# A residual turned by TensorE instead of by VectorE and a scratch in HBM

## The chip, the core and the metric

The kernel runs on one core of one Trainium2 chip. The time is what one execution takes on the device, in microseconds (us). A core has a matrix engine (TensorE, PE in the profile), three engines for elementwise work (VectorE or DVE, ScalarE or ACT, GpSimd or POOL), and a sync engine (SyncE or SP) that here only issues transfers (DMAs). Each engine runs its own list of instructions strictly in the listed order and waits on semaphores for the others. ACT issues DMAs too; such an instruction stands in ACT's list, and what is behind it waits for its turn. Data live in SBUF (128 partitions, the working memory), in PSUM (8 banks, where matmuls put their results) and in HBM.

## The reference, cut to what matters

The program is a two-layer decoder trunk on 512 tokens of width 1024. The change lies at its very end, in the last step of the last layer and the final norm:

```python
def per_layer_embed(h, p_i, g_norm, w_in, w_gate, b_gate):
    gate = jax.nn.sigmoid(rmsnorm(h, g_norm) @ w_gate + b_gate)
    return (p_i @ w_in) * gate
...
        h = h + conv_ffn(rmsnorm(h, norm_ffn[i]), f_w_up[i], f_conv_w[i], f_conv_b[i], f_w_down[i])
        h = h + per_layer_embed(h, p[i], norm_ple[i], ple_w_in[i], ple_w_gate[i], ple_b_gate[i])
...
    return rmsnorm(h, norm_final)
```

`h` is the residual. Its last use needs `h` twice: split into two parts as the operand of the gate matmul, and as itself in the addition `h + ...`.

## The kernel before

**Layout.** The residual is kept with features on the partitions: eight tiles `h[0]` to `h[7]`, each 128 features by 512 tokens. The last gate is computed the other way round, tokens on the partitions: four token blocks `i` of 128 tokens, each 1024 features wide, in two halves `c` of 512. So the residual has to be turned, from 8 tiles of features into 4 blocks of tokens (`hT[i][c]`), before the gate can be added to it.

**Matmuls in three products.** Each float32 operand is split into a high part that TensorE takes in its fast format and the low rest. A product of two split operands is three matmuls (`mm3`, L222 to L224, and `mm3t`, L233 to L235, which has tokens on the output's partitions). One gate half of one block is 8 x 3 = 24 matmuls of 128x512.

**Weights.** They come from HBM in units of 128x1024 (`load`, issued by SP into six buffers `r0` to `r5`), are cast to their high part by ACT (`wh`, L187) and have the rest taken by DVE (`wl`, L196), into four pairs of buffers `wh`/`wl`. A unit's cast needs its transfer and a free `wh` buffer; a transfer needs a free `r` buffer, that is the cast and the subtraction of the unit six places ahead. The names carry the unit's number: units 187 to 194 are the last down projection of the second layer, two for each quarter of the output; 195 to 198 are the gate's first half; 199 to 206, of 128x512, are its second half and go to buffers of their own (`own_ah`, `own_al`).

**The last down projection** (`dense_add`, L366) makes `d0` to `d7` in PSUM, 21 matmuls each. DVE adds each to the residual (`h`, L383); `norm.take` then has ACT make the high part of the gate's operand (`np10h`, L280) and its square (`np1sq`, L309), DVE the low part (`np10l`, L281), and POOL the running sum of squares (`np1acc`, L314). Behind this it calls `then`, which is `turn_h` (L963): DVE turns the tile within each 32x32 square (`ht`, a STREAM_TRANSPOSE, L966), and one tile later `write` (L956) issues four DMAs on ACT's list (L960), which put the squares to their places in a scratch `rows` in HBM. SP reads the scratch back as `hT` (L992), two transfers a block.

**The last gate** (`half` and `finish`, L1044 and L1053). `ms` is four small matmuls that put the tokens' sums of squares on the partitions; DVE and POOL make the root `rt` of it (L355, L357). For each half: matmuls into a PSUM bank `gate`, `z` on DVE (L1010, reads the bank, and needs `rt`), a sigmoid on ACT (`gs`, L1016), two operations on DVE (`gs` L1017 and `hT` L1019, which adds to the turned residual), a square with its sum on ACT (L1029). For each block: `total` on DVE (L1033, L1034), a root on POOL (`rfin`, L1039), a scaling on DVE (L1058); blocks 0 and 1 are turned back on DVE (L1064) and stored in sixteen DMAs (L1067), block 2 is stored as it is (L1061). The last block is cut finer: its second half is two quarters (`gate7`, `gate8`), and its end is the chain `z`, `gs`, `hT`, a sum on DVE (L1093), a root on POOL, a scaling on DVE and ACT (L1100, L1102), and two DMAs (L1103).

**What sets the order.** Code is written in program order, and a scheduler merges it into one list for each engine by priorities and by when it thinks that operands are ready. So an edit at one place can move instructions of others. PSUM tiles of one bank come from the tags `mm` (four banks), `tr` and `pv`; the pair of banks `sc` (`psum2`) exists once. Up to the first two tiles of the last down projection every engine's list is the same in both kernels.

Of the kernel before, what the change touches and what calls it, by code (L numbers as in the profile page):

```python
# [14 lines left out]
P = 128  # L15
# [37 lines left out]
def tile_yoco(ctx: ExitStack, tc: tile.TileContext, t, out: bass.AP, out_b: bass.AP):  # L53
# [18 lines left out]
    def psum2(name):  # L72
        return mmp.tile([P, 2, S], F32, tag="sc", name=name)
# [81 lines left out]
    def load(upto, queue=nc.sync):  # L155
        while state["raw"] < min(upto, len(units)):
            j = state["raw"]
            a, m, _ = units[j]
            tags = state["tags"]
            r = wp.tile([P, UNIT], F32, tag=f"r{tags[state['turn'] % len(tags)]}", bufs=1, name=f"wraw{j}")  # L160
            state["turn"] += 1
            if len(a.shape) == 4:
                for c in range(2):
                    queue.dma_start(r[:, :m].rearrange("p (k c n) -> p k c n", c=2, n=256)[:, :, c], a[:, :, c])
            else:
                queue.dma_start(r[:, :m], a)
            raws[j] = r
            state["raw"] += 1
# [57 lines left out]
    def mm3t(ps, xs, parts, c0, n, tok, first=True, last=True):  # L226

        for k, ((wh, wl, off), (xh, xl)) in enumerate(zip(parts, xs)):
            a, b = off + c0, off + c0 + n
            s = slice(tok * P, (tok + 1) * P)  # L230
            st = first and k == 0
            en = last and k == len(parts) - 1
            nc.tensor.matmul(ps, xh[:, s], wh[:, a:b], start=st, stop=False)  # L233
            nc.tensor.matmul(ps, xl[:, s], wh[:, a:b], start=False, stop=False)
            nc.tensor.matmul(ps, xh[:, s], wl[:, a:b], start=False, stop=en)  # L235
# [59 lines left out]
    class Norm:  # L295
# [56 lines left out]
    def inv_root(ms, name, scale=1.0):  # L352
        n = ms.shape[1]
        m = const.tile([P, n], F32, tag=f"ms{n}", bufs=2, name=f"{name}m")
        nc.vector.tensor_scalar(m, ms, scale, EPS, op0=ALU.mult, op1=ALU.add)  # L355
        r = const.tile([P, n], F32, tag=f"rt{n}", bufs=2, name=f"{name}rt")
        nc.gpsimd.tensor_tensor(r, m, minus_half[:, :n], op=ALU.pow)  # L357
        return r
# [7 lines left out]
    def dense_add(xs, kk, norm, fresh=False, then=None):  # L366

        for c in range(4):
            parts = chunk(256, kk)
            pss = []  # L370
            if fresh and c == 0:
                pss = [psum(f"d{j}") for j in range(2)]
                for k0, k1 in ((0, kk - 1), (kk - 1, kk)):
                    for j in range(2):
                        mm3(pss[j], parts[k0:k1], xs[k0:k1], j * P, first=k0 == 0, last=k1 == kk)
            for j in range(2):
                m = 2 * c + j
# [5 lines left out]
                nc.vector.tensor_add(h[m], h[m], ps)  # L383
                if norm is not None:
                    norm.take(m)
                if then is not None:
                    load(state["unit"] + RAWS)
                    then(m)

    def ffn(l, norm, nxt, then=None):  # L390
# [559 lines left out]
        nf.take(m)  # L950

    npl = Norm("np1", [(xp, "x", gain("norm_ple", 1))])
    rows = dram.tile([S, D], F32, name="rows")
    queue = []

    def write(m, t):  # L956

        for q in range(P // SQ):
            c0 = m * P + q * SQ
            nc.scalar.dma_start(rows[:, c0 : c0 + SQ].rearrange("(b i) j -> i b j", i=SQ),  # L960
                              t[q * SQ : (q + 1) * SQ, :].rearrange("p (b j) -> p b j", j=SQ))

    def turn_h(m):  # L963

        t = tp.tile([P, S], F32, tag=f"c{m % 2}", name=f"ht{m}")
        nc.vector.transpose(t, h[m])  # L966
        if queue:
            write(*queue.pop())
        queue.append((m, t))

    ffn(1, nf, npl, turn_h)
    write(*queue.pop())

    xs = npl.xs[0][0]
    brow, grow = (mp.tile([P, D], F32, tag=tag, name=f"row_{tag}") for tag in ("m4", "m5"))
    for i, r in enumerate((brow, grow)):
        nc.sync.dma_start(r.rearrange("p (m q) -> p m q", m=KD), lines[:, i, :].partition_broadcast(P))
    turned_h = at.tile([P, NC - 1, S], F32, tag="vd", name="hT")
    hT = [turned_h[:, q, :] for q in range(NC - 1)] + [at.tile([P, S], F32, tag="alibi", name="hT3")]
    hT = [hT[:2], hT[2:]]  # L980
# [63 lines left out]
    def half(i, c):  # L1044

        if c == 0 and i < 2:
            ps = pss[i]
        else:
            ps = psum(f"gate{i}_{c}")
            mm3t(ps, xs, parts2 if c else parts, 0, S, i)  # L1050
        square(i, gated(i, c * S, S, ps, c), c)

    def finish(i):  # L1053

        mean(i, 2, total[:, i : i + 1])
        r = root(i)
        for c in range(2):
            nc.vector.scalar_tensor_tensor(hT[i][c], hT[i][c], r, grow[:, c * S : (c + 1) * S],  # L1058
                                           op0=ALU.mult, op1=ALU.mult)
            if i == 2:  # L1060
                nc.sync.dma_start(out_b[0, :, c * S : (c + 1) * S], hT[i][c])  # L1061
                continue
            t = tp.tile([P, S], F32, tag=f"c{c}", name=f"y{i}_{c}")
            nc.vector.transpose(t, hT[i][c])  # L1064
            for q in range(P // SQ):
                s0 = i * P + q * SQ
                nc.sync.dma_start(flat[c * S : (c + 1) * S, s0 : s0 + SQ].rearrange("(f c) a -> c f a", c=SQ),  # L1067
                                  t[q * SQ : (q + 1) * SQ, :].rearrange("p (f a) -> p f a", a=SQ))
# [101 lines left out]
```

## Time and profile before

| | us |
|---|---|
| median of three runs | 1144.76 (1144.58 to 1144.79) |
| the profiled execution | 1144.59 |
| its span, first to last instruction | 1142.9 |
| PE busy | 1123.6 (98%) |
| DVE busy | 736.2 (64%) |
| ACT busy | 505.4 (44%) |
| POOL busy | 134.6 (12%) |
| TensorE clock granted, mean | 0.994 |

The profiled execution lies within the runs; 1.69 us of its time are outside its span. A row of the timeline has the start in us from the span's beginning, the duration in us, the engine, the line of the kernel, the operation, and output `<-` inputs by the program's names; "x4" is four merged into one row, and in brackets stands the time the engine sat idle before it and whose work ended that. "ACTq" and "SPq" are the parts of ACT and SP that issue DMAs. A matmul's duration overlaps that of the next: what it costs is the distance from its start to the next start. PEclk is the granted TensorE clock, 1.00 at full speed.

### The profile page before, as it was taken

To read this page: it belongs to the slowest core of one execution; us is meant where nothing else is said; L and a number is where in the kernel's file an instruction comes from. 1 tells how busy PE (TensorE), PEld (TensorE's weight loads), DVE (VectorE), ACT (ScalarE), POOL (GpSimd) and SP (SyncE) were. 2 spreads that over 40 slices of the span, in tenths; PEclk is the share of its full clock that TensorE was granted. 3 is DMA by queue.
4 is the path that set the end of the run, shared out by engine and by line. 5 is a ranking of instruction groups with operands and counts; after the bars stand their busy time and mean duration, and the time that the engine had idled before them with its cause. 6 is when DMAs were issued, how large, how long until landed. Compare 5 with 4: busy or idle time off the path is not lost.

```text
span 1142.9 us, 13466 instructions
## 1 busy us (share of the span) xinstructions
PE 1123.6 (98%) x5116; PEld 932.2 (82%) x5116; DVE 736.2 (64%) x974; ACT 505.4 (44%) x801; POOL 134.6 (12%) x160
## 2 busy tenths in 40 slices
PE   9999999999999999999999999999999999999895
PEld 7888888888888888888898887888888888888675
DVE  7356467762677367557858887677636773677556
ACT  6533344441343244445756776544413432344342
POOL 2100210000000000022235564100000000000101
PEclk9999999999999999999999999999999999999998
DMA  9322322322323333332054324433223233323443
GB/s 319 110 94 81 104 89 96 111 92 92 109 69 100 111 109 88 99 111 94 18 147 129 93 93 166 136 104 111 86 98 103 73 102 111 102 70 113 90 124 74
DMA packets 70097, 120.66 MB, mean 106 GB/s; under 512 B 30344, under 2 KB 41104, under 8 KB 70032
## 3 DMA queue, kind: packets, MB, share of 16 engines
q1 hardware_dynamic: 52704, 117.24, 32.5%
q10 hardware_dynamic: 17328, 2.56, 1.2%
q8 instruction: 40, 0.66, 0.2%
q14 instruction: 25, 0.20, 0.1%
HBM read 110.33 MB, written 4.20 MB: 100 GB/s over the span
## 4 chain that ended last, share of the span: by engine, by line
PE 93%; DVE 2%; DMA 1%; issue 1%; ACT 1%; ACTq 0%; SPq 0%; POOL 0%; POOLq 0%
PE up L222 14%; PE up L224 14%; PE up L223 14%; PE d L224 8%; PE d L223 8%; PE d L222 8%; PE o L222 1%; PE q L222 1%; PE o L223 1%; PE o L224 1%; PE sc L738 1%; PE q L224 1%; PE gate L222 1%; PE q L223 1%; PE u L222 1%
## 5 line engine op out<-in xcount | busy, mean ns | idle before, releaser
L196 DVE TENSOR_TENSOR wl<-wraw,wh 128x1024 fp32r<-128x1024 f32 (+2 forms) x197 | 239.5, 1218 | 117.9 <-ACT wh L187 117.3
L187 ACT CAST wh<-wraw 128x1024 fp32r<-128x1024 f32 (+1 forms) x196 | 201.7, 1032 | 245.9 <-PE d L223 132.8
L224 PE MATMUL d<-ah,wl 128*128 128x512 f32 x352 | 137.8, 391 | 2.2 <-DVE wl L196 2.2
L223 PE MATMUL d<-al,wh 128*128 128x512 f32 x352 | 137.6, 391 | 0.0
L222 PE MATMUL d<-ah,wh 128*128 128x512 f32 x352 | 137.5, 391 | 0.0
L222 PE MATMUL up<-nf00h,wh 128*128 128x512 f32 x352 | 137.1, 390 | 0.0
L222 PE MATMUL up<-nf10h,wh 128*128 128x512 f32 x352 | 137.0, 389 | 0.0
L224 PE MATMUL up<-nf00h,wl 128*128 128x512 f32 x352 | 137.0, 389 | 0.0
L223 PE MATMUL up<-nf00l,wh 128*128 128x512 f32 x352 | 136.9, 389 | 0.0
L224 PE MATMUL up<-nf10h,wl 128*128 128x512 f32 x352 | 136.9, 389 | 0.0
L223 PE MATMUL up<-nf10l,wh 128*128 128x512 f32 x352 | 136.9, 389 | 0.0
L412 ACT ACTIVATE c<-hs,vec 128x512 f32<-128x512 f32 x88 | 71.8, 816 | 88.9 <-DVE hs L408 87.9
L413 DVE SCALAR_TENSOR_TENSOR c<-hs,vec,c 128x511 f32<-128x511 f32 x88 | 65.9, 748 | 37.4 <-ACT c L412 37.2
L383 DVE TENSOR_TENSOR h<-h,d 128x512 f32<-128x512 f32 x56 | 38.4, 686 | 79.7 <-PE d L224 79.7
L224 PEld LDWEIGHTS d<-ah,wl 128*128 128x128 f32 x352 | 66.4, 189 | 16.4 <-DVE wl L196 2.6
L222 PEld LDWEIGHTS d<-ah,wh 128*128 128x128 f32 x352 | 66.5, 189 | 13.9
L223 PEld LDWEIGHTS d<-al,wh 128*128 128x128 f32 x352 | 66.4, 189 | 13.9
L284 ACT CAST ah<-a 128x512 fp32r<-128x512 f32 x44 | 27.4, 622 | 113.5 <-DVE a L418 113.5
L224 PEld LDWEIGHTS up<-nf10h,wl 128*128 128x128 f32 x352 | 66.1, 188 | 13.8
L222 PEld LDWEIGHTS up<-nf00h,wh 128*128 128x128 f32 x352 | 66.1, 188 | 13.7
L223 PEld LDWEIGHTS up<-nf00l,wh 128*128 128x128 f32 x352 | 66.1, 188 | 13.7
L223 PEld LDWEIGHTS up<-nf10l,wh 128*128 128x128 f32 x352 | 66.1, 188 | 13.7
(289 smaller groups left out, 1976.1 us busy)
## 6 DMA issues: line engine op xcount, KB each, us to landing
wraw<-in_w_up SPq DMA_DIRECT2D x88, 512.0 KB, 3.5
wraw<-in_w_down SPq DMA_DIRECT2D x32, 512.0 KB, 3.5
wraw<-in_w_down SPq DMA_DIRECT2D x16, 384.0 KB, 3.3
wraw<-in_w_u SPq DMA_DIRECT2D x8, 512.0 KB, 7.7
wraw<-in_w_out SPq DMA_DIRECT2D x8, 512.0 KB, 3.5
wraw<-in_w_gate SPq DMA_DIRECT2D x8, 512.0 KB, 3.8
wraw<-in_w_q SPq DMA_DIRECT2D x8, 512.0 KB, 3.5
wraw<-in_w_o SPq DMA_DIRECT2D x8, 512.0 KB, 3.2
```

The costliest lines, as they stand in the source:

```text
L187: nc.scalar.copy(wh[:, :n], src)
L196: nc.vector.tensor_sub(wl[:, :n], src, wh[:, :n].bitcast(F32))
L222: nc.tensor.matmul(ps, wh[:, a:b], xh, start=st, stop=False)
L223: nc.tensor.matmul(ps, wh[:, a:b], xl, start=False, stop=False)
L224: nc.tensor.matmul(ps, wl[:, a:b], xh, start=False, stop=en)
L284: nc.scalar.copy(hi, src)
L383: nc.vector.tensor_add(h[m], h[m], ps)
L412: nc.scalar.activation(c, hs, AF.Identity, bias=v("conv_b", l * 2 * NJ + col), scale=cw[2])
L413: nc.vector.scalar_tensor_tensor(c[:, 1:], hs[:, : S - 1], cw[1], c[:, 1:], op0=ALU.mult, op1=ALU.add)
L738: nc.tensor.matmul(o[:, e, 2 * P - nk :], q, x[g // 2][:, g % 2, t0 : t0 + nk], start=st, stop=not st)
```

## The change

The turned residual is made another way. `turn_h`, `write`, the scratch `rows` and the eight reads of it are gone. In their place a new `turn_h(i)` turns one token block: eight TensorE transposes (a matmul with the identity, 128x128 each, in float32), one from each `h[k]`, into the pair of banks `sc`, and one ACT copy of 128x1024 from there to SBUF. It is called once ahead of the gate's second halves (block 0) and then behind the second half of block `i` for block `i + 1`. Since `sc` exists once, a block's transposes wait for the copy of the block before.

What comes with it: `dense_add` no longer calls `load` ahead of `then`; `ms` moves from `sc` to the bank `tr`; the blocks of the gate are now run one after the other (first half, second half, finish) and not both first halves first; the turned block lies in buffers `r3` to `r5`; and the output of blocks 0 and 1 is turned into one tile of 128x1024 and stored in eight DMAs of double size instead of sixteen.

```diff
@@ dense_add
                 if then is not None:
-                    load(state["unit"] + RAWS)
                     then(m)
@@ behind the last attention
-    rows = dram.tile([S, D], F32, name="rows")
-    queue = []
-
-    def write(m, t):
-
-        for q in range(P // SQ):
-            c0 = m * P + q * SQ
-            nc.scalar.dma_start(rows[:, c0 : c0 + SQ].rearrange("(b i) j -> i b j", i=SQ),
-                              t[q * SQ : (q + 1) * SQ, :].rearrange("p (b j) -> p b j", j=SQ))
-
-    def turn_h(m):
-
-        t = tp.tile([P, S], F32, tag=f"c{m % 2}", name=f"ht{m}")
-        nc.vector.transpose(t, h[m])
-        if queue:
-            write(*queue.pop())
-        queue.append((m, t))
-
-    ffn(1, nf, npl, turn_h)
-    write(*queue.pop())
+    ffn(1, nf, npl)
...
-    for i in range(2):
-        r = wp.tile([P, D], F32, tag=f"r{4 + i}", bufs=1, name=f"hT{2 + i}")
-        hT.append([r[:, :S], r[:, S:]])
-    for i in range(NC):
-        for c in range(2):
-            nc.sync.dma_start(hT[i][c], rows[i * P : (i + 1) * P, c * S : (c + 1) * S])
-    ms = psum2("ms")[:, 0, :NC]
+    full += [wp.tile([P, D], F32, tag=f"r{2 + i}", bufs=1, name=f"hT{i}") for i in range(1, NC)]
+    hT = [[x[:, :S], x[:, S:]] for x in full]
+    def turn_h(i):
+
+        ps = psum2(f"ht{i}")
+        for k in range(KD):
+            nc.tensor.transpose(ps[:, k // 4, k % 4 * P : (k % 4 + 1) * P], h[k][:, i * P : (i + 1) * P], ident)
+        nc.scalar.copy(full[i], ps.rearrange("p a s -> p (a s)"))
+
+    ms = psum("ms", "tr")[:, :NC]
...
     rt = inv_root(ms, "np1", 1.0 / D)
+    turn_h(0)
@@ half
             mm3t(ps, xs, parts2 if c else parts, 0, S, i)
+        if c and i < end:
+            turn_h(i + 1)
         square(i, gated(i, c * S, S, ps, c), c)
@@ finish
-            t = tp.tile([P, S], F32, tag=f"c{c}", name=f"y{i}_{c}")
-            nc.vector.transpose(t, hT[i][c])
+            nc.vector.transpose(t[:, c * S : (c + 1) * S], hT[i][c])
+        if i < 2:
...
     for i in range(2):
-        half(i, 0)
-    for i in range(2):
-        half(i, 1)
+        for c in range(2):
+            half(i, c)
         finish(i)
```

Three places show what this does to the lists. A name here is the tile's, with its own number behind an underscore.

The first is DVE's list in the last down projection, where the low parts of the weights for `d6` and `d7` are made (`wl193`, `wl194`). Before:

```order
L383 TENSOR_TENSOR h4_84<-h4_84,d4_8500 128x512
L966 STREAM_TRANSPOSE ht4_8535<-h4_84 128x512
L281 SCALAR_TENSOR_TENSOR np10l3_6020<-h3_83,vec_79,np10h3_6019 128x512
L383 TENSOR_TENSOR h5_85<-h5_85,d5_8541 128x512
L966 STREAM_TRANSPOSE ht5_8570<-h5_85 128x512
L196 TENSOR_TENSOR wl193_8493<-wraw193_8383,wh193_8492 128x1024
L196 TENSOR_TENSOR wl194_8497<-wraw194_8385,wh194_8496 128x768
```

After:

```order
L383 TENSOR_TENSOR h2_82<-h2_82,d2_8397 128x512
L281 SCALAR_TENSOR_TENSOR np10l2_6018<-h2_82,vec_79,np10h2_6017 128x512
L196 TENSOR_TENSOR wl193_8458<-wraw193_8455,wh193_8457 128x1024
L383 TENSOR_TENSOR h3_83<-h3_83,d3_8426 128x512
L196 TENSOR_TENSOR wl194_8464<-wraw194_8461,wh194_8463 128x768
L281 SCALAR_TENSOR_TENSOR np10l3_6020<-h3_83,vec_79,np10h3_6019 128x512
L196 TENSOR_TENSOR own199_al4_8658<-wraw199_8654,own199_ah4_8657 128x512
L383 TENSOR_TENSOR h4_84<-h4_84,d4_8467 128x512
L196 TENSOR_TENSOR own200_al5_8665<-wraw200_8661,own200_ah5_8664 128x512
L281 SCALAR_TENSOR_TENSOR np10l4_6022<-h4_84,vec_79,np10h4_6021 128x512
L196 TENSOR_TENSOR wl195_8529<-wraw195_8525,wh195_8528 128x1024
L383 TENSOR_TENSOR h5_85<-h5_85,d5_8496 128x512
```

`wl193` stood behind the addition `h5`, which needs `d5`, the matmuls just ahead of those that need `wl193`; it now stands ahead of `h3`. In the same way `wl195`, for the gate's first matmuls, stood behind `h7` and now stands ahead of `h5`.

The second is ACT's list where the down projection ends. Before:

```order
L309 ACTIVATE np1sq6_8609<-h6_86 128x512
L960 DMA rows_6029<-ht5_8570 32x16x32 x4
L280 ACTIVATE np10h7_6027<-h7_87,vec_79 128x512
L309 ACTIVATE np1sq7_8650<-h7_87 128x512
L960 DMA rows_6029<-ht6_8619 32x16x32 x4
L960 DMA rows_6029<-ht7_8654 32x16x32 x4
L187 CAST wh197_8670<-wraw197_8445 128x1024
L187 CAST wh198_8674<-wraw198_8448 128x1024
L187 CAST own199_ah4_8716<-wraw199_8529 128x512
```

After:

```order
L309 ACTIVATE np1sq6_8564<-h6_86 128x512
L187 CAST own202_ah7_8678<-wraw202_8675 128x512
L187 CAST wh197_8605<-wraw197_8602 128x1024
L187 CAST own205_ah1_8699<-wraw205_8696 128x512
L187 CAST own206_ah2_8706<-wraw206_8703 128x512
L187 CAST wh198_8612<-wraw198_8609 128x1024
L280 ACTIVATE np10h7_6027<-h7_87,vec_79 128x512
L309 ACTIVATE np1sq7_8593<-h7_87 128x512
L187 CAST own203_ah8_8685<-wraw203_8682 128x512
L187 CAST own204_ah0_8692<-wraw204_8689 128x512
```

The casts of units 197 and 198 stood behind eight writes of the scratch and now stand ahead of the work on `h7`; most casts of the gate's second half have moved into the down projection.

The third is PE's list where the gate's second half begins. Before, block 0's second half followed block 1's first half at once, and the first twelve matmuls of the last block (`gate3_0`) stood further ahead, before `ms`:

```order
L233 MATMUL gate1_8679<-wh198_8674,np10h7_6027 128x512
L234 MATMUL gate1_8679<-wh198_8674,np10l7_6028 128x512
L235 MATMUL gate1_8679<-wl198_8675,np10h7_6027 128x512
L233 MATMUL gate0_1_8811<-own199_ah4_8716,np10h0_6013 128x512
L234 MATMUL gate0_1_8811<-own199_ah4_8716,np10l0_6014 128x512
```

After:

```order
L235 MATMUL gate1_8617<-wl198_8613,np10h7_6027 128x512
L972 MATMUL ht0_8734<-ident_131,h0_80 128x128
L972 MATMUL ht0_8734<-ident_131,h1_81 128x128
L972 MATMUL ht0_8734<-ident_131,h2_82 128x128
L972 MATMUL ht0_8734<-ident_131,h3_83 128x128
L972 MATMUL ht0_8734<-ident_131,h4_84 128x128
L972 MATMUL ht0_8734<-ident_131,h5_85 128x128
L972 MATMUL ht0_8734<-ident_131,h6_86 128x128
L972 MATMUL ht0_8734<-ident_131,h7_87 128x128
L233 MATMUL gate0_1_8756<-own199_ah4_8657,np10h0_6013 128x512
L234 MATMUL gate0_1_8756<-own199_ah4_8657,np10l0_6014 128x512
```

The transposes of blocks 1, 2 and 3 stand behind `gate0_1`, `gate1_1` and `gate2_1` in the same way, and `gate3_0` now runs whole behind the last of them.

More of the change, by code (lines that the diff above doesn't have):

```diff
@@ L978, in tile_yoco @@
     turned_h = at.tile([P, NC - 1, S], F32, tag="vd", name="hT")
-    hT = [turned_h[:, q, :] for q in range(NC - 1)] + [at.tile([P, S], F32, tag="alibi", name="hT3")]
-    hT = [hT[:2], hT[2:]]
+    full = [turned_h[:, :2, :].rearrange("p a s -> p (a s)")]
     parts = chunk(S, KD)
@@ L1056, in finish @@
         r = root(i)
+        t = wp.tile([P, D], F32, tag=f"r{i}", bufs=1, name=f"y{i}") if i < 2 else None
         for c in range(2):
@@ L1062, in finish @@
                 continue
-            t = tp.tile([P, S], F32, tag=f"c{c}", name=f"y{i}_{c}")
-            nc.vector.transpose(t, hT[i][c])
+            nc.vector.transpose(t[:, c * S : (c + 1) * S], hT[i][c])
+        if i < 2:
             for q in range(P // SQ):
                 s0 = i * P + q * SQ
-                nc.sync.dma_start(flat[c * S : (c + 1) * S, s0 : s0 + SQ].rearrange("(f c) a -> c f a", c=SQ),
+                nc.sync.dma_start(flat[:, s0 : s0 + SQ].rearrange("(f c) a -> c f a", c=SQ),
                                   t[q * SQ : (q + 1) * SQ, :].rearrange("p (f a) -> p f a", a=SQ))
     for i in range(2):
-        half(i, 0)
-    for i in range(2):
-        half(i, 1)
+        for c in range(2):
+            half(i, c)
         finish(i)
```

## The prediction

> **What bounds the kernel now.** I read the page first, then the busy time by stretches of the last 100 us, then the timelines of PE, DVE, ACT and SP there. The page says that PE is the engine to look at:
>
> ```profile
> PE 1123.6 (98%) x5116; PEld 932.2 (82%) x5116; DVE 736.2 (64%) x974; ACT 505.4 (44%) x801; POOL 134.6 (12%) x160
> ```
>
> What PE does not use of the span is small, and most of it lies in two stretches of 14 us (columns: stretch, its length, busy time of PE, PEld, DVE, ACT, POOL, then granted clock, DMA share and GB/s):
>
> ```profile
> 1049.00:1068.00 19.00, 19.00 (x85) 15.58 (x83) 10.51 (x15) 8.19 (x13) 5.25 (x4) 1.00 0.51 111
> 1068.00:1082.00 14.00, 11.63 (x43) 8.97 (x42) 7.57 (x9) 4.38 (x6) 2.86 (x2) 0.88 0.47 112
> 1082.00:1096.00 14.00, 11.20 (x45) 8.97 (x46) 6.54 (x10) 5.29 (x8) 1.33 (x1) 0.88 0.40 95
> ```
>
> Up to 1068 PE is full at clock 1.00; in the next two stretches it idles and its clock falls to 0.88. PE's timeline shows three stalls:
>
> ```profile
> 1067.83 0.39 PE L223 MATMUL d<-al,wh 128*128 128x512 f32 x1
> 1070.40 0.50 PE L224 MATMUL d<-ah,wl 128*128 128x512 f32 x1 [2.18 <-DVE wl L196]
> ...
> 1074.62 0.40 PE L223 MATMUL d<-al,wh 128*128 128x512 f32 x1
> ...
> 1080.97 0.39 PE L224 MATMUL d<-ah,wl 128*128 128x512 f32 x1
> 1081.20 0.39 PE L233 MATMUL gate<-wh,np10h 128*128 128x512 f32 x1
> 1081.43 0.39 PE L234 MATMUL gate<-wh,np10l 128*128 128x512 f32 x1
> 1083.99 0.50 PE L235 MATMUL gate<-wl,np10h 128*128 128x512 f32 x1 [2.18 <-DVE wl L196]
> ...
> 1088.21 0.39 PE L234 MATMUL gate<-wh,np10l 128*128 128x512 f32 x1
> ...
> 1094.57 0.40 PE L234 MATMUL gate<-wh,np10l 128*128 128x512 f32 x1
> 1095.78 0.50 PE L235 MATMUL gate<-wl,np10h 128*128 128x512 f32 x1 [0.81 <-DVE wl L196]
> ...
> 1131.01 0.28 PE L235 MATMUL gate<-own_al,np10h 128*128 128x256 f32 x1
> ```
>
> An undisturbed matmul costs 0.227 us (1080.97, 1081.20, 1081.43). **Stall A**: 1067.83 to 1070.40 is 2.57, less 0.23 is 2.34; the eleven matmuls from 1070.40 to 1074.62 then take 4.22 instead of 2.50, 1.72 more, since the clock has fallen. Together 4.06. **Stall B**, at the gate's first low part: 2.56 less 0.23, and again 4.22 for eleven from 1083.99 to 1088.21: 4.05. **Stall C**: 1.21 less 0.23, 0.98, with no slow matmuls behind it. Sum 9.09 us. All three end with a `wl` on DVE. Why it is late, DVE shows:
>
> ```profile
> 1067.81 0.69 DVE L383 TENSOR_TENSOR h<-h,d 128x512 f32<-128x512 f32 x1 [2.69 <-PE d L224]
> 1068.53 0.71 DVE L966 STREAM_TRANSPOSE ht<-h 128x512 f32<-128x512 f32 x1
> 1069.17 3.14 DVE L196 TENSOR_TENSOR wl<-wraw,wh 128x1024 fp32r<-128x1024 f32 x2
> ...
> 1081.40 0.69 DVE L383 TENSOR_TENSOR h<-h,d 128x512 f32<-128x512 f32 x1 [2.69 <-PE d L224]
> 1082.12 0.71 DVE L966 STREAM_TRANSPOSE ht<-h 128x512 f32<-128x512 f32 x1
> 1082.76 2.32 DVE L196 TENSOR_TENSOR wl<-wraw,wh 128x1024 fp32r<-128x1024 f32 x2
> ...
> 1094.51 2.35 DVE L196 TENSOR_TENSOR wl<-wraw,wh 128x1024 fp32r<-128x1024 f32 x2
> ```
>
> In A and B the subtraction stands in DVE's list behind an addition that waits for the matmuls just before (idle 2.69), and behind the transpose. DVE was free; the order held it. In C the list of ACT held it:
>
> ```profile
> 1086.31 5.60 ACTq L960 DMA_DIRECT2D rows<-ht  x8
> 1091.95 1.99 ACT L187 CAST wh<-wraw 128x1024 fp32r<-128x1024 f32 x2 [8.59 <-DMA rows<-ht]
> ...
> 1102.63 0.62 ACT L187 CAST own_ah<-wraw 128x512 fp32r<-128x512 f32 x1 [1.17 <-DMA wraw<-in_w_gate]
> ```
>
> Eight scratch writes take ACT's list 5.60 us, the casts of units 197 and 198 come behind them, and the last weights, whose buffers these casts free, are issued late by SP:
>
> ```profile
> 1095.75 3.84 SPq L164 DMA_DIRECT2D wraw<-in_w_gate  x8
> ```
>
> **What sets the end** is not PE's last matmul but DVE's chain behind it:
>
> ```profile
> 1114.93 0.71 DVE L1010 SCALAR_TENSOR_TENSOR z<-gate,np1rt,row_m 128x512 f32<-128x512 f32 x1
> ...
> 1122.17 0.71 DVE L1010 SCALAR_TENSOR_TENSOR z<-gate,np1rt,row_m 128x512 f32<-128x512 f32 x1
> ...
> 1124.91 0.74 DVE L1010 SCALAR_TENSOR_TENSOR z<-gate,np1rt,row_m 128x512 f32<-128x512 f32 x1
> ...
> 1133.01 1.39 DVE L1019 TENSOR_TENSOR hT<-hT,gs 128x256 f32<-128x256 f32 x1
> ...
> 1135.29 0.47 DVE L1010 SCALAR_TENSOR_TENSOR z<-gate,np1rt,row_m 128x256 f32<-128x256 f32 x1
> ```
>
> The last `z` starts at 1135.29, 4.28 behind the start of the last matmul, though an addition that waits for PE starts only 0.43 behind it (1080.97 to 1081.40). For a 256 wide matmul, 0.28 long and not 0.39, that is 0.32. DVE is about 4 us late here: the gate began late for it, since the last casts came at 1102.63. From the last `z` to the end of the span are 7.61 us, which the change does not touch.
>
> **The change, part by part.**
>
> *Removed.* Eight transposes on DVE (0.71 each, 5.7 us), 32 writes on ACT's list, eight reads on SP's. With them go the reasons for C. A and B go because the new lists have `wl193` ahead of `h3` and `wl195` ahead of `h5`, an output tile or more ahead of the matmuls that need them. So PE gains 9.09. What is late next there: `wl197`, needed by the gate's thirteenth matmul. Without stall A the gate begins at 1081.20 - 4.06 = 1077.14, and the thirteenth is due at 1079.86. Its `wh` buffer is free after twelve matmuls of `d7` (1075.1); behind it stand the cast of unit 202 (0.62), its own cast (half of 1.99) and a subtraction (half of 2.35): about 1078.0. Slack 1.9 us. I cost it at nothing; if the slack fails, at one stall (4.05).
>
> *Weights without the early `load`.* SP's list has the same transfers in the same order up to unit 200, each waiting only for its buffer, so nothing starts later. Units 203 and 204 wait for `wl197` and `wl198`, now near 1080.7. Eight transfers took 1095.75 to 1102.63, 6.9 us, to their last cast; two units should need less, so by 1087.6 at worst, and `gate0_1` needs them from its thirteenth matmul, near 1091.5. Cost nothing.
>
> *Added on PE.* 32 transposes. The attention step has the same operation, four at a time between 128x512 matmuls:
>
> ```profile
> 601.50 0.60 PE L782 MATMUL tr<-ident,prs 128*128 128x128 f32 x4
> 601.86 0.48 PE L222 MATMUL q<-n11h,wh 128*128 128x512 f32 x1
> 602.17 0.40 PE L223 MATMUL q<-n11l,wh 128*128 128x512 f32 x1
> ...
> L782 PE MATMUL tr<-ident,prs x64: 270/272/274, 601.5 to 688.2; 128*128 128x128 f32 x64
> ```
>
> Four of them and one matmul take 0.67, less 0.227 is 0.44, or 0.11 each. Eight groups of four: 3.52. Bounds: 0.09 each if only 601.50 to 601.86 counts (2.9), and the whole 272 ns each if they do not overlap in longer runs (8.7). I take 0.11, the same instruction in the same surroundings.
>
> By the Trainium skill, "TensorE: Matmul & The Clock Gate", Part 4 (PE-mode transpose), a transpose took about 275 ns in one kernel's context and does not count as activity that keeps the clock up. Its duration agrees with the 272 ns here, but the starts here are 0.11 apart. By 275 ns as a price the sum would come out 5.3 us later.
>
> *Added on ACT.* Four copies of 128x1024 from PSUM, bounded by these two groups:
>
> ```profile
> L797 ACT CAST pp<-tr 128x512 fp32r<-128x512 f32 x8 | 4.7, 587 | 4.5 <-PE tr L782 4.5
> ```
>
> Two of those are 1.17, the 128x1024 cast above is 1.00; I take 1.05. ACT has room (4.48 busy of the 19.5 us before 1131.5):
>
> ```profile
> 1112.00:1131.50 19.50, 19.29 (x108) 16.78 (x106) 14.48 (x25) 4.48 (x10) 1.44 (x3) 1.00 0.34 59
> ```
>
> *The wait added.* `sc` exists once, so `ht1` on PE waits for the copy of `ht0`, and behind `ht1` stands the rest of the gate. In ACT's list that copy stands behind the first sigmoid, which needs `z`, which needs the root `rt`:
>
> ```profile
> 1094.67 1.93 POOL L357 TENSOR_TENSOR np1rt<-np1m,minus_half 128x4 f32<-128x4 f32 x1 [13.82 <-DVE np1m L355]
> ```
>
> `ms` is done near 1077.14 + 42 x 0.227 + 0.8 = 1087.5; with 0.2 for DVE, 1.93 for POOL, 0.74 for `z`, 0.63 for the sigmoid and 1.05 for the copy it ends near 1092.4 to 1093.4. `ht1` is due after 72 gate matmuls, `ms` (0.9) and eight transposes (0.88): 1095.2. Slack about 2 us; for the later blocks it is more. Cost nothing.
>
> *The new order of the blocks.* A block costs PE 48 x 0.227 + 0.88 = 11.8 us and DVE 10.0: 7.24 from the `z` of a second half through the block's finish to the next block's first `z` (1114.93 to 1122.17), 2.74 from that to the second (1124.91). So DVE no longer falls behind; PE sets the pace, and the last `z` starts when its bank is ready. Stores of double size lie behind DVE's work and end long before the last ones: nothing.
>
> *Sum.* PE's last matmul starts at 1131.01 - 9.09 + 3.52 = 1125.44, the last `z` at 1125.76. That is 9.53 earlier than 1135.29. The profiled execution took 1144.59, so 1135.06; it lies 0.17 below the median of the runs, so by that 1135.2. I forecast 1135.1, 0.8% faster.
>
> **Rivals.** (1) *One stall comes back elsewhere* (unit 197, or a copy that holds PE): 4.06 more, 1139.2. For it: slacks of 2 us are short, and a DVE subtraction can take longer than 1.2 (the two at 1069.17 took 3.14). Against it: a miss below 1 us costs only itself, as C shows. (2) *The transposes do not overlap* in runs of eight: 8.70 instead of 3.52, 1140.3. Against it: four in a row do. (3) *The transposes count as idleness* and the clock falls after each block: four times 1.72, 1142.0. Against it: the fall came after 2.3 us of stall, not after the 0.98 of C, and a group is 0.88 long. It is what the Trainium skill's rule on PE-mode transposes, quoted above, would bring. (4) *The other side: the last weights come no earlier.* Units 203 and 204 stand in DVE's list ahead of `np1m`, so of `rt`, of the first `z`, and so of the copy that `ht1` waits for. Were their casts at 1102.63 as now, then 0.7 for the subtraction, 0.2, 1.93, 0.74, 0.63 and 1.05 put the copy's end at 1108.5 and `ht1` 13.3 late: 1148.4, slower. It costs from about 1091.5 on and cancels the gain if they land near 1099. Against it: what held them was the row of writes on ACT.
>
> **Chances.** The forecast 0.70, (1) 0.12, (2) 0.07, (3) 0.04, (4) 0.05, two of (1) to (3) together 0.02. A measurement here can tell 0.2%, 2.3 us, from no change: faster is all of the forecast, (1), (2) and nearly all of (3), 0.92; the same 0.03; slower 0.05. Range: the forecast's own is 1133.5 to 1137. Below it reaches to 1132.8, where the transposes cost a third of what I took, above to 1139.4, which takes in (1); that leaves out (2) to (4), 0.18.
>
> **What would show it.** PE without idle time between 1040 and its last matmul, at clock 1.00; a last matmul near 1125.4; the eight transposes of a block within 0.9 us; the first `z` near 1090 and not 1101.24; about 0.3 us from the last matmul's start to the last `z`. Wrong would be: a wait on `wh197` or on a copy in PE's list, slow matmuls behind the transposes, or casts of units 203 and 204 after 1091.

## The result, and the profile after

The changed kernel takes 1134.66 us, the median of four runs (1134.41 to 1134.97); the kernel before, run beside it, 1144.67 (1143.23 to 1144.79). The ratio is 0.9921, with a 95% interval of 0.9907 to 0.9935. The profiled execution took 1134.84 us, with a span of 1133.1 against 1142.9.

The page of the changed kernel, busy time by engine:

```profile
PE 1122.9 (99%) x5148; PEld 933.4 (82%) x5148; DVE 730.4 (64%) x966; ACT 509.7 (45%) x805; POOL 134.1 (12%) x160
```

PE is as busy as before, within 0.7 us, but with other work: the slow matmuls behind stalls A and B (1.72 us more each) are gone, and 32 transposes (3.48) have come. Beside this, what went is its idle time. The two stretches that showed the stalls, and the one that holds the last matmul (stretch, length, busy time of PE, PEld, DVE, ACT, POOL, granted clock, DMA share, GB/s):

```profile
1068.00:1082.00 14.00, 14.00 (x63) 11.58 (x63) 10.62 (x13) 8.75 (x14) 3.08 (x2) 1.00 0.22 63
1082.00:1096.00 14.00, 14.00 (x75) 11.87 (x74) 4.83 (x8) 4.28 (x7) 1.02 (x1) 1.00 0.05 13
...
1112.00:1125.60 13.60, 13.60 (x87) 12.16 (x85) 8.68 (x16) 5.16 (x12) 2.42 (x3) 1.00 0.32 71
```

PE is full and its clock is 1.00, where before it was busy for 11.63 and 11.20 of 14 us at 0.88. The timeline of DVE shows why, and how the end follows PE:

```profile
1057.09 1.23 DVE L196 TENSOR_TENSOR wl<-wraw,wh 128x1024 fp32r<-128x1024 f32 x1 [1.35 <-ACT wh L187]
1058.27 0.69 DVE L383 TENSOR_TENSOR h<-h,d 128x512 f32<-128x512 f32 x1
...
1076.92 1.21 DVE L196 TENSOR_TENSOR wl<-wraw,wh 128x1024 fp32r<-128x1024 f32 x1
...
1088.93 0.75 DVE L993 SCALAR_TENSOR_TENSOR z<-gate,np1rt,row_m 128x512 f32<-128x512 f32 x1 [1.14 <-POOL np1rt L357]
...
1113.56 0.75 DVE L993 SCALAR_TENSOR_TENSOR z<-gate,np1rt,row_m 128x512 f32<-128x512 f32 x1 [0.34 <-PE gate L235]
...
1119.89 0.75 DVE L993 SCALAR_TENSOR_TENSOR z<-gate,np1rt,row_m 128x512 f32<-128x512 f32 x1 [0.20 <-PE gate L235]
...
1125.75 0.15 DVE L1017 TENSOR_SCALAR others<-others 128x1 f32<-128x1 f32 x1
1125.82 0.47 DVE L993 SCALAR_TENSOR_TENSOR z<-gate,np1rt,row_m 128x256 f32<-128x256 f32 x1
```

The subtraction of unit 193 now starts at 1057.09, ahead of an addition, and not at 1069.17 behind `h5`. The first `z` starts at 1088.93 (before: 1101.24), and the last at 1125.82 (before: 1135.29). Some `z` wait for PE, by 0.34 and 0.20. PE's own rows give the price of a block's transposes and the last matmul:

```profile
1088.69 0.39 PE L235 MATMUL gate<-wl,np10h 128*128 128x512 f32 x1
1088.92 1.03 PE L972 MATMUL ht<-ident,h 128*128 128x128 f32 x8
1089.71 0.48 PE L233 MATMUL gate<-own_ah,np10h 128*128 128x512 f32 x1
1090.02 0.40 PE L234 MATMUL gate<-own_ah,np10l 128*128 128x512 f32 x1
...
1125.32 0.28 PE L235 MATMUL gate<-own_al,np10h 128*128 128x256 f32 x1
```

From 1088.92 to 1090.02 is 1.10; less one matmul of 0.227 that is 0.87 for eight, 3.48 for the four blocks.

The span shrank by 9.8: PE's last matmul starts 5.69 earlier (1131.01 to 1125.32), the last `z` follows it after 0.50 instead of 4.28 (3.78), and from there to the end are 7.28 instead of 7.61 (0.33).

### The profile page after: what moved, and what is told of

Same layout as the page of the kernel before. It is cut to its first block, busy times and chain, and to the rows that moved or that the text cites. A ratio compares the mean times of both kernels' runs of the same rounds, so it can differ in the third digit from the quotient of the medians.

```text
span 1133.1 us, 13468 instructions
## 1 busy us (share of the span) xinstructions
PE 1122.9 (99%) x5148; PEld 933.4 (82%) x5148; DVE 730.4 (64%) x966; ACT 509.7 (45%) x805; POOL 134.1 (12%) x160
## 4 chain that ended last, share of the span: by engine, by line
PE 98%; DMA 0%; DVE 0%; issue 0%; ACT 0%; SPq 0%; POOL 0%; POOLq 0%; ACTq 0%
PE up L222 14%; PE up L223 14%; PE up L224 14%; PE d L222 8%; PE d L223 8%; PE d L224 8%; PE o L222 1%; PE o L223 1%; PE q L222 1%; PE o L224 1%; PE sc L737 1%; PE q L224 1%; PE gate L222 1%; PE q L223 1%; PE u L224 1%; PE u L222 1%
## 5 line engine op out<-in xcount | busy, mean ns | idle before, releaser
L224 PEld LDWEIGHTS up<-nf00h,wl 128*128 128x128 f32 x352 | 66.1, 188 | 13.8
```

Source lines behind the costliest of these rows:

```text
L224: nc.tensor.matmul(ps, wl[:, a:b], xh, start=False, stop=en)
```

## The experiments

The expectations speak of one theory and three rivals. *Theory 1*: the scratch writes in ACT's list hold ACT and push the subtractions of units 193 and 195 behind `h5` and `h7`; the gain is stalls A, B and C and DVE's lag, less PE's transposes. *Rival 2*: the traffic of the scratch, thousands of small packets, made the stalls. *Rival 3*: the eight transposes on DVE made them. *Rival 4*: the gain is in what came along, the order of the blocks or the early `load`. All times below are medians. Runs of the kernel before stand beside each of them on the same chip (medians 1143.66 to 1144.13); the changed kernel was not run again there, so a difference of some tenths from its 1134.66 tells nothing.

### Put DVE's transposes back, without the writes

```diff
-    ffn(1, nf, npl)
+    def turn_old(m):
+        t = tp.tile([P, S], F32, tag=f"c{m % 2}", name=f"old{m}")
+        nc.vector.transpose(t, h[m])
+    ffn(1, nf, npl, turn_old)
```

> The changed kernel with the eight DVE transposes of h put back; their result is used by nothing, and there are no scratch writes. Theory 1 (the writes in ACT's list hold ACT and push the subtractions of units 193 and 195 behind h5 and h7; the gain is stalls A, B and C and DVE's lag, less PE's transposes): the subtractions keep their places, DVE has room, PE stays full: 1134.7, at most 1135.3. Rival 3 (the 5.7 us of transposes on DVE made the stalls): about 4 to 6 us more, 1139 to 1141.

1135.07 us (1134.72 to 1135.61); ratio to before 0.9922, interval 0.9909 to 0.9934. In the stretch that held stall A, DVE works 2.5 us more than in the changed kernel and PE stays full:

```profile
1068.00:1082.00 14.00, 14.00 (x64) 11.58 (x63) 13.13 (x17) 8.67 (x13) 2.88 (x2) 1.00 0.20 57
```

Rival 3 falls: DVE's transposes were hidden work.

### Put the writes back too, in ACT's list

```diff
+    rows = dram.tile([S, D], F32, name="rows")
+    queue = []
+    def write(m, t):
+        for q in range(P // SQ):
+            c0 = m * P + q * SQ
+            nc.scalar.dma_start(rows[:, c0 : c0 + SQ].rearrange("(b i) j -> i b j", i=SQ),
+                              t[q * SQ : (q + 1) * SQ, :].rearrange("p (b j) -> p b j", j=SQ))
```

(Left out here: `turn_old` also queues the tile for `write`, one tile late, as the kernel before does.)

> As the run with the DVE transposes, and the 32 scratch writes are put back in ACT's list; nobody reads the scratch. Theory 1: the subtractions stand behind h5 and h7 again, so stalls A and B (4.06 and 4.05) and C (0.98) are back while PE keeps its own transposes: 1134.7 + 9.1 = 1143.8; up to 4 us more if DVE falls behind again as well, down to 1142.8 if C alone stays away. Rival 2 (the traffic of the small packets made the stalls): the same. Rival 3: 1139 to 1141.

1141.90 us (1141.43 to 1143.47): 7.2 us of the gain are gone with 32 DMA instructions whose data nobody reads. In DVE's list the subtractions of units 193 and 194 stand behind the addition `h5` again:

```profile
1067.95 0.69 DVE L383 TENSOR_TENSOR h<-h,d 128x512 f32<-128x512 f32 x1 [2.70 <-PE d L224]
...
1069.31 3.15 DVE L196 TENSOR_TENSOR wl<-wraw,wh 128x1024 fp32r<-128x1024 f32 x2
```

All three stalls are back at PE:

```profile
1068.70 0.33 PE L991 MATMUL ht<-ident,h 128*128 128x128 f32 x1 [0.23 <-DVE h L383]
...
1070.55 0.50 PE L224 MATMUL d<-ah,wl 128*128 128x512 f32 x1 [1.06 <-DVE wl L196]
...
1080.70 0.33 PE L991 MATMUL ht<-ident,h 128*128 128x128 f32 x1 [0.67 <-DVE h L383]
...
1082.55 0.50 PE L235 MATMUL gate<-wl,np10h 128*128 128x512 f32 x1 [1.05 <-DVE wl L196]
...
1094.35 0.50 PE L235 MATMUL gate<-wl,np10h 128*128 128x512 f32 x1 [0.81 <-DVE wl L196]
```

A and B are shorter than 2.18 because the scheduler now puts the eight transposes of block 0 into them (the rows of L991), and in the profiled execution the clock fell behind B alone (1.00 from 1068 to 1082, 0.88 from 1082 to 1096). So 1143.8, which counts two falls, was too high: by 1.9 against the median, by 0.5 against the profiled execution, which took 1143.25. Since rival 2 expected the same, this run does not tell it from theory 1. In the profiled execution PE's last matmul starts 6.94 later than in the changed kernel, and the last `z` 1.87 behind it.

### The same writes, issued by POOL

The edit is `nc.gpsimd.dma_start` in place of `nc.scalar.dma_start`.

> As the run with the writes in ACT's list, with the same 32 writes issued by POOL. The packets in the DMA engines are the same, but nothing stands in ACT's list, and the subtractions of units 193 and 195 keep their early places. Theory 1: 1134.7 to 1136. Rival 2 (the traffic of the small packets): about as the run with the writes on ACT, 1142 to 1144.

1138.23 us (1137.77 to 1139.01), 3.6 slower than the changed kernel, which neither expectation holds. PE does what theory 1 says:

```profile
1068.00:1082.00 14.00, 14.00 (x63) 11.61 (x62) 12.65 (x16) 8.60 (x14) 11.69 (x17) 1.00 0.51 130
```

It stays full in this stretch, and its last matmul starts at 1125.06. The 3.6 us are lost behind it. ACT's list puts block 0's sigmoid behind three copies:

```profile
1102.39 1.02 ACT L992 COPY hT<-ht 128x1024 f32<-128x1024 f32 x1 [5.31 <-PE ht L991]
...
1104.73 1.15 ACT L1018 ACTIVATE gs<-z 128x512 f32<-128x512 f32 x2
```

Block 0 is added up from 1105.39 on instead of 1090.38, and DVE's last `z` comes at 1128.41, 3.35 behind PE. Nor was the traffic the same, as I had written: POOL's queue moved the 2.10 MB in 1,024 packets, where ACT's needs some 16,900. So this run does not decide on rival 2.

### The kernel before, with its writes issued by SP

```diff
-            nc.scalar.dma_start(rows[:, c0 : c0 + SQ].rearrange("(b i) j -> i b j", i=SQ),
+            nc.sync.dma_start(rows[:, c0 : c0 + SQ].rearrange("(b i) j -> i b j", i=SQ),
```

> The kernel before, with its 32 scratch writes issued by SP. The packets are those of before, in a queue of the hardware; ACT's list is free of them and the subtractions of units 193 and 195 stand early, but SP's list now holds the last weights back. Theory 1: PE has no stall between 1049 and the gate (A and B gone), and a stall or two of some us in the gate for the last eight weights: 1137 to 1141. Rival 2 (the traffic of the packets): stalls A and B stay, 1144 or more.

This one decides. In DVE's list the subtraction of unit 193 stands early, ahead of an addition:

```profile
1057.37 1.28 DVE L196 TENSOR_TENSOR wl<-wraw,wh 128x1024 fp32r<-128x1024 f32 x1 [0.95 <-ACT wh L187]
1058.58 0.68 DVE L383 TENSOR_TENSOR h<-h,d 128x512 f32<-128x512 f32 x1
```

The page counts the packets of the kernel before to the last one:

```profile
DMA packets 70097, 120.66 MB, mean 105 GB/s; under 512 B 30344, under 2 KB 41104, under 8 KB 70032
```

and the stretches show no stall, at a DMA share of 0.69 where the kernel before had 0.51:

```profile
1049.00:1068.00 19.00, 19.00 (x85) 15.73 (x85) 14.67 (x19) 9.78 (x15) 5.32 (x4) 1.00 0.69 153
1068.00:1082.00 14.00, 14.00 (x64) 11.59 (x63) 13.09 (x16) 8.86 (x12) 2.87 (x2) 1.00 0.35 76
1082.00:1096.00 14.00, 14.00 (x68) 11.72 (x67) 7.06 (x13) 4.27 (x8) 1.02 (x1) 1.00 0.60 169
```

Rival 2 falls. PE's last matmul starts at 1122.04, 9.0 us earlier than before, which is the 9.09 that the prediction gave for the three stalls. And yet the run takes 1147.54 us (1146.95 to 1148.03), slower than before, where I had expected 1137 to 1141. The number lies in the "1144 or more" of rival 2, but the stalls that should have made it are not there. DVE stands idle behind PE's list:

```profile
1113.97 0.75 DVE L1010 SCALAR_TENSOR_TENSOR z<-gate,np1rt,row_m 128x512 f32<-128x512 f32 x1 [17.81 <-PE gate L235]
```

PE's list mixes the second halves of the blocks here, and the next bank that DVE's list asks for is complete only at 1113.9. That the late weights on SP's list make the scheduler do so is likely, but was not tried. Most of DVE's work on the blocks is then still to be done; its last `z` is 13.67 behind PE. And from there to the end of the span are 10.3 us, not 7.61: SP issues the last block's store at 1142.39, 2.89 behind ACT's, where the two were 0.06 apart before.

### The kernel before, with its writes issued by POOL; and with the new order of blocks as well

The first edit is the one above with `nc.gpsimd`; the second adds

```diff
     for i in range(2):
-        half(i, 0)
-    for i in range(2):
-        half(i, 1)
+        for c in range(2):
+            half(i, c)
         finish(i)
```

> The kernel before, with its 32 scratch writes issued by POOL in place of ACT; DVE's transposes, the scratch, its reads and the order of the blocks stay. With the writes out of ACT's list the subtractions of units 193 and 195 stand early, as in the changed kernel, and PE has no transposes. Theory 1: stalls A, B and C are gone and PE's last matmul starts near 1131.0 - 9.1 = 1121.9; with DVE at most 2 us behind, 1131.5 to 1133.5, faster than the changed kernel. If the gain needs the scratch itself to go (rival 2, or the reads of it on SP): 1140 or more.

> As the kernel before with the writes on POOL, and with the changed kernel's order of the blocks (both halves of a block, then its finish). Theory 1: PE's last matmul near 1121.9, the blocks cost PE 10.9 us and DVE 10.0, so DVE keeps up: 1131.5 to 1132.5. If the order does not matter: the same as with the old order.

1146.19 (1143.84 to 1148.48) and 1144.14 us (1142.10 to 1146.19), both far above the times of theory 1. The first lies in the "1140 or more" of the other side, but not for its reason, since the stalls are gone. PE's last matmul starts at 1123.03 and 1123.22, as theory 1 has it (a wait of 1.2 us for `np1acc` makes it 1.1 late), but the last `z` at 1131.51 and 1130.46, and the end of the span is another 10.6 and 9.9 us behind it, with SP's last store late again. In the first of them:

```profile
1101.28 0.75 DVE L1010 SCALAR_TENSOR_TENSOR z<-gate,np1rt,row_m 128x512 f32<-128x512 f32 x1 [4.69 <-PE gate L235]
1101.94 0.68 DVE L1017 TENSOR_TENSOR gs<-gs,pet 128x512 f32<-128x512 f32 x1
1112.38 0.75 DVE L1010 SCALAR_TENSOR_TENSOR z<-gate,np1rt,row_m 128x512 f32<-128x512 f32 x1 [9.76 <-PE gate L235]
1113.05 0.68 DVE L1019 TENSOR_TENSOR hT<-hT,gs 128x512 f32<-128x512 f32 x1
```

A `z` that is not ready stands in DVE's list ahead of additions that have long been. PE took the second half of block 2 ahead of its first half, so that `z` became ready only at 1112. Both profiled executions were the fastest of their runs, which reach 4.6 and 4.1 us higher; what those runs lost no trace shows. With this spread, the 2.05 us between the two medians do not tell much of the order of the blocks.

### The order of the blocks alone, and the early load alone

The first is the second edit above on the kernel before; the other takes `load(state["unit"] + RAWS)` out of it.

> The kernel before with the new order of the blocks alone. Theory 1: the stalls stay and the gate starts no earlier, so DVE's work behind its first z at 1101 is the same and it stays about 4 us late: 1143.5 to 1144.7. Rival 4 (the order of the blocks is what removes DVE's lag): PE's last matmul at 1131.0, the last z 0.3 behind it, 1140.6.

> The kernel before without the early load call alone. Theory 1: SP's transfers stand in the same order and wait for the same buffers, so no difference: 1143.5 to 1144.7. Rival 4 (the early load is a part of the stalls or of the gain): more than 1 us either way.

Without the early load: 1144.60 us, ratio 1.0002 (0.9993 to 1.0011), no difference. The new order alone: 1142.30 us (1140.90 to 1143.31), ratio 0.9984 (0.9975 to 0.9992), which is neither of the two numbers. The stalls are there (PE waits 2.18, 2.18 and 0.81 for `wl`), but the last `z` comes at 1131.78, 2.24 behind PE's last matmul at 1129.54, not 4.28. So rival 4 holds in part: the order of the blocks is worth 2.0 us of DVE's lag by itself (1.8 us of time against the kernel before).

### Twice the transposes on PE

```diff
-        for k in range(KD):
+        for k in [x for x in range(KD) for _ in range(2)]:
             nc.tensor.transpose(ps[:, k // 4, k % 4 * P : (k % 4 + 1) * P], h[k][:, i * P : (i + 1) * P], ident)
```

> The changed kernel with each of the 32 PE transposes done twice (64). By the price taken from the attention step (0.11 each) and with PE's last matmul setting the end: 3.5 us more, 1138.2. If the groups were hidden or something else set the end: 1134.7. If they count as idleness once a group is 1.8 us long and the clock falls behind each: 3.5 and up to 4 x 1.72 more, 1145.

1138.58 us (1138.13 to 1138.68), 3.9 more than the changed kernel.

```profile
1089.26 1.91 PE L972 MATMUL ht<-ident,h 128*128 128x128 f32 x16
1090.92 0.48 PE L233 MATMUL gate<-own_ah,np10h 128*128 128x512 f32 x1
1091.23 0.40 PE L234 MATMUL gate<-own_ah,np10l 128*128 128x512 f32 x1
```

Sixteen cost 1.97 less 0.23, 1.74, twice the 0.87. Four blocks make 3.48 of the 3.83 by which PE's last matmul is later; the other 0.34 is there already at the first transpose (1089.26 against 1088.92). The end follows PE, and matmuls behind 1.7 us of transposes run at full clock.

### A version without PE's transposes, its lists bound

If PE's transposes cost 3.5 us and DVE's nothing, the detour through HBM with the writes on POOL should beat the changed kernel, once the lists behind the gate are in a good order. On the changed kernel:

```diff
+    for i in range(NC):
+        nc.sync.dma_start(full[i], rows[i * P : (i + 1) * P, :])
...
-    turn_h(0)
...
-        if c and i < end:
-            turn_h(i + 1)
...
+    with in_order(*engines[1:]):
+        for i in range(2):
+            for c in range(2):
+                half(i, c)
+            finish(i)
```

with the old `turn_h` and `write` (on POOL); `in_order` binds DVE, ACT and POOL to the written order (left out here: blocks 2 and 3 stand in it too). The second kernel is this without `in_order`. The third binds another order: the first halves of blocks 0 and 1 come first, and each `z` ahead of the finish of the block before.

> The changed kernel, with h turned by DVE and the scratch again (its 32 writes issued by POOL, four reads of a whole block each on SP) in place of TensorE's transposes and ScalarE's copies, and with the gate's blocks bound to the written order on DVE, ACT and POOL. The run with the writes on POOL had PE free of stalls A, B and C and lost 8 us behind PE, since DVE's list held block 0's sums behind a later block's z. Theory 1, with the order of DVE's list behind the gate as its second half: PE's last matmul starts near 1122 to 1123, DVE follows within 1 us, 1131.5 to 1133: 2 to 3 us faster than the changed kernel. If DVE cannot keep pace with a gate that has no transposes in it, whatever its order: 1136 or more.

> The same without the bound order: DVE's, ACT's and POOL's lists behind the gate as the scheduler makes them. Theory 1 with the order as its second half: PE as in the run with the bound order, DVE 6 to 9 us behind: 1139 to 1144. If the order of the list is not what costs there: as with the bound order, within 1 us.

> As the run with the bound order, but the order bound on DVE, ACT and POOL is another: the first halves of blocks 0 and 1 come first, and each z stands ahead of the finish of the block before it. In the run with the bound order PE ended at 1121.6 and DVE's last z came 4.0 later, with DVE idle in block 0 (2.8 us for PE) and 2.9 us a block in waits for ACT's sigmoid, ACT's square and POOL's root. If the order of DVE's list is what costs there, this order fills these waits: last z at 1122 to 1123, and 7.4 to its end and 1.9 outside the span: 1131.5 to 1132.5, faster than the changed kernel. If DVE's work itself is too much for a gate without transposes: no better than 1135.

The three take 1135.40 us (1135.01 to 1136.00) with the order bound, 1136.56 (1136.33 to 1136.96) with the scheduler's, and 1136.70 (1136.61 to 1137.34) with the other bound order. None beats the changed kernel, against what I expected of the first and the third. The first equals it within the noise (0.9927 of the kernel before, interval 0.9914 to 0.9939), and lies between the two numbers expected of it; the third came as "no better than 1135". The scheduler's order costs 1.2 us against the bound one, not the 6 or more that I expected of the second. PE ends 3.7 to 3.9 us earlier in each of them, and DVE does not. The first, PE and then DVE:

```profile
1121.59 0.28 PE L235 MATMUL gate<-own_al,np10h 128*128 128x256 f32 x1
```

```profile
1101.92 0.71 DVE L1006 SCALAR_TENSOR_TENSOR z<-gate,np1rt,row_m 128x512 f32<-128x512 f32 x1
...
1112.20 0.71 DVE L1006 SCALAR_TENSOR_TENSOR z<-gate,np1rt,row_m 128x512 f32<-128x512 f32 x1
...
1125.56 0.47 DVE L1006 SCALAR_TENSOR_TENSOR z<-gate,np1rt,row_m 128x256 f32<-128x256 f32 x1
```

A block takes DVE 10.28 us here, 2.9 of them in waits for ACT and POOL, and the last `z` stands at 1125.56, where the changed kernel has it at 1125.82. The third kernel fills these waits with the next `z`, and loses more by it:

```profile
1110.79 0.75 DVE L1006 SCALAR_TENSOR_TENSOR z<-gate,np1rt,row_m 128x512 f32<-128x512 f32 x1 [5.26 <-PE gate L235]
```

This `z` is the first half of block 2. PE's rows just before it say why it is late: PE works on the second half's weights (`own`) up to 1104.70, and only then on the first half's (`wh`):

```profile
1104.70 0.39 PE L235 MATMUL gate<-own_al,np10h 128*128 128x512 f32 x1
1104.92 0.61 PE L233 MATMUL gate<-wh,np10h 128*128 128x512 f32 x2
```

The scheduler has again put block 2's second half first, and binding DVE, ACT and POOL did not bind PE. A kernel that binds PE's order as well was not tried, so whether the detour can beat TensorE's transposes stays open.

## Why the prediction was right

- **Stalls A, B and C (9.09).** They went, through the path that the prediction named: with the writes out of ACT's list the subtractions stand early (moved to SP: PE 9.0 us earlier with all packets kept; put back in ACT's list: the stalls return). What the prediction had wrong is that it took the slow matmuls (1.72 behind A, 1.72 behind B) as a fixed part of each stall. Of 64 runs of the kernel before beside the experiments, 29 had a mean granted clock of 0.995 or 0.996 and a median of 1143.0 us, and 35 one of 0.993 or 0.994 and 1144.55: 1.55 apart, about one fall of the clock. The execution that I took my terms from had two falls. The changed kernel, without stalls, varies by 0.6 us. The time forecast does not hang on this, since the execution that it starts from has both falls in it.
- **What held the subtractions.** In A and B it was DVE's order, as the prediction says, and not ACT at that moment: the casts were done at 1062.80 and 1078.28, 5.0 and 3.1 us before the additions (1067.81 and 1081.40) behind which the subtractions stood.

```profile
1061.01 1.79 ACT L187 CAST wh<-wraw 128x1024 fp32r<-128x1024 f32 x2 [0.75 <-issue]
...
1076.28 2.00 ACT L187 CAST wh<-wraw 128x1024 fp32r<-128x1024 f32 x2 [6.51 <-DMA rows<-ht]
```

  So the writes acted through the order that the scheduler makes; why it puts the subtractions behind the additions was not looked into. In C the prediction has ACT's list as the cause, and that is only a part. DVE's list held this subtraction as well, behind `np1m`, which waits for PE:

```profile
1094.43 0.16 DVE L355 TENSOR_SCALAR np1m<-ms 128x4 f32<-128x4 f32 x1 [7.43 <-PE ms L998]
```

  The cast of unit 197, half of 1.99 us from 1091.95, was done near 1092.95, and the subtraction started at 1094.51, 1.6 us later. Started at 1092.95 and as long as here (half of 2.35), it would have ended near 1094.1 by this estimate, before the 1094.80 at which PE wanted it.
- **32 transposes on PE (3.52).** Measured 3.48, and doubled they cost as much again. Rivals (2) and (3), no overlap or a falling clock, did not come: a group of eight costs 0.87 us, and the clock behind it is 1.00. The Trainium skill, "TensorE: Matmul & The Clock Gate", Part 4 (PE-mode transpose), has about 275 ns for one and says that it does not count as activity. Each lasts 272 ns here, but eight of them cost 0.87 us together; and groups of 0.87 and 1.74 us did not lower the clock, so what the rule on activity would do to a longer run of them no run here shows.
- **PE's last matmul.** Forecast 1125.44, measured 1125.32.
- **DVE's lag (3.96).** Measured 3.78, but the reason that the prediction gives for the lag, that the gate began late for DVE, was half of it. The order of the blocks alone takes 2.0 of the 4.28 away. With that order and the stalls back the lag is still 1.87; the rest goes with them.
- **"PE sets the pace".** True by a narrow margin. The last `z` comes 0.50 behind the last matmul's start and not 0.32: by 0.32 its bank was ready at 1125.64, and DVE's own `others`, which stands ahead of it, starts at 1125.75. In the version without PE's transposes PE ends 3.7 us earlier and the time is the same, so DVE is close behind; but PE's list has the halves in another order there, which is part of it.
- **What was costed at nothing.** `wl197` is done at 1078.13 (forecast 1078.0, due at 1079.86). The last of units 203 and 204 is cast at 1084.46 (forecast: subtracted by 1087.6 at worst). The first copy ends early, mainly since the root before it took 1.02 and not 1.93:

```profile
1084.46 0.62 ACT L187 CAST own_ah<-wraw 128x512 fp32r<-128x512 f32 x1 [2.35 <-DMA wraw<-in_w_gate]
...
1090.25 1.00 ACT L973 COPY hT<-ht 128x1024 f32<-128x1024 f32 x1
```

  It is done at 1091.25 (forecast 1092.4 to 1093.4), and `ht1` starts at 1095.25 (forecast 1095.2) without a wait. The four copies took 1.00 to 1.02 each (forecast 1.05). So rivals (1) and (4) did not come.
- **The tail (unchanged).** 7.28 instead of 7.61. On the engines it is the same, 3.79 and 3.78 from the last `z` to ACT's last DMA; the 0.33 lie between that DMA and the end of the span.
- **The sum.** 1135.06 was forecast for the profiled execution, which took 1134.84. The errors were 0.12 at PE and 0.33 in the tail, both to the faster side, and 0.18 at DVE and 0.05 outside the span to the other.

## What to carry to other kernels

A DMA in the list of a computing engine is an instruction of that engine, and where a scheduler orders the lists it moves the others too: here 32 of them cost PE 9 us through subtractions on a third engine, so read what stands ahead of the instruction that ends a wait before blaming traffic or load. A full matrix engine does not set the end by itself: seven of these kernels had PE without its three stalls and lost 3 to 14 us behind it, in several, by their rows, because half blocks were made in an order that the engine behind could not use. The distance from the last matmul to the instruction that reads its bank, and the order in which banks become complete, show that at once.

## What the runs showed of the hardware that I had not expected

**The clock falls in some executions and not in others, behind the same stall.** In the run with the new order of the blocks alone, PE waits 2.18 us at stall A, as in the kernel before, and the matmuls behind it stay 0.23 apart:

```profile
1070.51 0.50 PE L224 MATMUL d<-ah,wl 128*128 128x512 f32 x1 [2.18 <-DVE wl L196]
1070.85 0.39 PE L222 MATMUL d<-ah,wh 128*128 128x512 f32 x1
1071.08 0.39 PE L223 MATMUL d<-al,wh 128*128 128x512 f32 x1
```

In the kernel before, the matmuls behind the same wait stand 0.43 apart for about 3.4 us, beginning 0.6 us after the stall. And in the run with the writes back in ACT's list, waits of only 0.67 and 1.05 us, 1.85 apart, were followed by such a fall, where in no profile here the single 0.81 of stall C was, nor the single 1.20 and 1.39 us for `np1acc` in the runs with the writes on POOL. The Trainium skill, "TensorE: Matmul & The Clock Gate", Part 1 (What's actually happening), describes a free-running window of about 3.4 us by which the clock is set: the length of the falls and their chance agree with it. Its condition for the fall, one idle window or more, does not agree: PE's waits here are 2.18 us and less.

**A GpSimd root of 128x4 depends on what runs beside it.** It took 1.93 us in the kernel before, beside two subtractions on DVE, and here 1.02, beside nothing on DVE. The 1.93 comes in the three other runs with the subtractions beside it, and 1.02 to 1.04 in the nine others without:

```profile
1087.87 1.02 POOL L357 TENSOR_TENSOR np1rt<-np1m,minus_half 128x4 f32<-128x4 f32 x1 [11.43 <-DVE np1m L355]
```

The Trainium skill, "SBUF — State Buffer", Who interferes with whom, names a pair of ports that GpSimd shares with VectorE and that is locked by one of them at a time. These two durations agree with it.

**The issuing engine decides how many packets a write has.** The same 32 writes of 32x16x32 squares make some 16,900 packets from ACT or SP and 1,024 from POOL, where each takes about 0.64 us of POOL's list.
